# Later places in the engines' queues for three pieces of work, and other loads and layouts in a retention and sparse-attention block

## Chip, cores, metric

The kernel runs on one core of a Trainium2 chip. The metric is the time of one execution on the device in microseconds (us), the median of several runs. A profile of one execution comes with it: the span of its instructions, the busy time of each engine, and what each engine waited for. The engines are called PE (TensorE, matrix products), PEld (its weight loads), DVE (VectorE), ACT (ScalarE), POOL (GpSimd) and SP (SyncE, which here only issues DMAs).

## The reference, cut to what matters

One layer over 1,024 tokens of width 1,024, all in float32:

```
h    = rms_norm(x)                      # needs the sum of squares of each token
proj = h @ w_in                         # columns split between two token mixers
group A: q, k rotated; ret = retention(q, k, v)   # 8 heads, chunk-causal, decay per head
         ret = head_group_norm(ret) * silu(gate_a)
group B: score[t, s] = sum_h w[t, h] * relu(qi[t, h] . ki[s])   # the indexer, 8 heads
         keep the 256 best keys of each token; softmax attention over these alone,
         keys and values from a latent c_kv (rms-normalised, width 128) through w_uk, w_uv
         dsa = attention * silu(gate_b)
x = x + concat(ret, dsa) @ w_out
x = x + sigmoid(rms_norm(x) @ w_ple_gate) * (p @ w_ple_proj);  out = rms_norm(x)
```

The rotations need tables of cos and sin of position times frequency, one for the retention heads (`cosr`, `sinr`) and one for the sparse group (`cosx`, `sinx`).

## The kernel before, in words

Matrix products in full float32 precision are made of three fast ones: each operand is split into a high part (ACT copies it to the fast format, `xhi`, `whi`) and a rest (`xlo` by DVE, `wlo` by POOL). The work goes through these stages.

1. **Start.** For each of 8 slices of x: load, split (L257, L258), square on ACT, add to `acc` on DVE (L266). PE runs the first projection (L300 to L302) on the slices. On DVE the angle tables (L331 to L339, a range reduction of nine steps for each of the two tables) have no place of their own: they stand between the slices' work. When `acc` is complete, PE sums it over the partitions (L365), `rsqrt` gives `rstd`, `spread` copies it to all partitions (`rstd_b`), and DVE multiplies the tables with it and rotates the first projection (L382 to L401). The rotated indexer queries and keys go to DRAM (`d_iq`, `d_ik`), with the rotary part of the attention queries (`d_qs`) and keys (`d_kp`), all issued on SP's queue.
2. **Indexer scores** (L449 to L455), six token tiles in the order 7, 6, 4, 2, 3, 5: load `qs` from `d_iq`, 8 products per tile, relu on ACT, weighted sum on DVE. Tiles 0 and 1 need no scores.
3. **Column chunks** (`n_chunk`, L472 to L474, PE work that needs only x and weights) in the order 2, 3, 0, 1: 8 token tiles each with 24 products per tile. Then `t_block`s (L310 to L312): the retention queries and keys (rotated on DVE into `d_f`), the latent (block 8, squares on ACT at L523, their sum over partitions on PE at L526), and the attention queries (blocks 9 to 11, into `d_qs`). Then chunks 4 and 5.
4. **The search for the 256th score**, bit by bit, beside stage 3: rows 2, 3, 5 on DVE (L624), rows 7, 6, 4 on ACT (L640), then `narrow` and `choose` (L685 to L689) on DVE, which write the mask `bias`.
5. **Keys and values** from the latent: `prep_v` and `prep_k` (L726 to L745); DVE makes the rests at L731 and L745. They use the memory of x and its weights, so they come when chunk 5 is done. `start_block` loads the queries `ql`, `qh` from `d_qs` into the memory of the scores, so it comes when the search is done.
6. **Retention** in 8 halves (4 head pairs, 2 halves of the sequence), two in flight, beside the attention of query blocks 0 and 1. `retention_load` fetches mask `mk`, `qk`, `vt` and gate `gt`; `retention_out` multiplies with the gate and stores to `d_mix`.
7. **Attention** of blocks 2 and 3, beside the two output projections (`project`), the gate products and the final norm.

Each engine executes its instructions in the order of its queue, and so do the DMA issues of SP. That order isn't written by hand: a scheduler at build time makes it from priorities (mostly the order in the program) and from its own estimate of when each operand is ready. A tile pool hands out buffers in that order and makes the next user wait for the last.

Of the kernel before, what the change touches and what calls it, by code (L numbers as in the profile page):

```python
# [153 lines left out]
def _body(ctx, nc, tc, ap, dbg):  # L154
    V, A, G, T, Y = nc.vector, nc.scalar, nc.gpsimd, nc.tensor, nc.sync

    def f(t):
        return t.bitcast(F32)

    def pool(name, **kw):  # L160
        return tc.tile_pool(name=name, bufs=kw.pop("bufs", 1), reuse_waits="tile", **kw)
# [28 lines left out]
    d_iq = dram.tile([2, 32, 8, S], F32, name="d_iq")  # L190
    d_qs = dram.tile([2, 64, 8, S], F32, name="d_qs")
    d_f = [dram.tile([128, 2, S], F32, name=f"d_f{g}") for g in range(4)]
# [67 lines left out]
    def add_squares(k):  # L260
        raw = raws[k // 2][:, k % 2]
        if k == 0:
            A.activation(acc, raw, AF.Square)
        else:
            A.activation(raw, raw, AF.Square)
            V.tensor_tensor(out=acc, in0=acc, in1=raw, op=OP.add)  # L266

# [8 lines left out]
    for k in range(NT):  # L276
# [7 lines left out]
        if k > 0:  # L284
            add_squares(k - 1)
    add_squares(NT - 1)
    Y.dma_start(same, ap["cst"][:, CF:CN])
# [16 lines left out]
    def t_block(b, outs):  # L304
        ws = [load_w(ap["w_t"][b, kg], 128) for kg in range(2)]
        for h in range(2):
            sl = slice(512 * h, 512 * h + 512)
            for k in range(NT):
                wh, wl = (t[:, k % 4] for t in ws[k // 4])
                T.matmul(outs[h], wh, xhi[k][:, sl], start=k == 0, stop=False)  # L310
                T.matmul(outs[h], wh, xlo[k][:, sl], start=False, stop=False)  # L311
                T.matmul(outs[h], wl, xhi[k][:, sl], start=False, stop=k == 7)  # L312

# [30 lines left out]

    angles(1, cosx)
    tables(cosx, sinx)
    angles(0, cosr)

# [64 lines left out]
    for n in range(2):  # L413
        Y.dma_start(d_qs[n, 0:16].rearrange("(x j) h t -> (j h) x t", x=2), f(xs[n])[0:64])
        Y.dma_start(d_kp[n].rearrange("(x j) t -> j x t", x=2), f(xs[n])[104:112])
# [16 lines left out]
    for i in TI:  # L432
# [7 lines left out]
        for h in range(8):  # L440
# [5 lines left out]
            for b0, b1, pb in pbs:  # L446
                for c0 in range(b0, b1, 512):
                    c1 = min(b1, c0 + 512)
                    T.matmul(pb[:, c0 - b0:c1 - b0], qs[:, h], ks[:, c0:c1], start=True, stop=True)  # L449
                A.activation(rel[:, b0:b1], pb[:, :b1 - b0], AF.Relu, scale=32.0 ** -0.5)  # L450
# [10 lines left out]
    def n_chunk(c, func, place=nb):  # L461
        ws = [load_w(ap["w_n"][c, kg], 256) for kg in range(4)]
        for tg in range(2):
            for a in range(4):
# [5 lines left out]
                for k in range(NT):  # L470
                    wh, wl = (t[:, k % 2] for t in ws[k // 2])
                    T.matmul(pb[:, a % 2], xhi[k][:, tsl], wh, start=k == 0, stop=False)  # L472
                    T.matmul(pb[:, a % 2], xhi[k][:, tsl], wl, start=False, stop=False)  # L473
                    T.matmul(pb[:, a % 2], xlo[k][:, tsl], wh, start=False, stop=k == 7)  # L474
                A.activation(st[:, a % 2], pb[:, a % 2], func, scale=rstd[:, j:j + 1])  # L475
# [49 lines left out]
    for j in range(NT):  # L525
        T.matmul(pk[:, j:j + 1], cq[:, 128 * j:128 * j + 128], ones1, start=True, stop=True)  # L526
    rkv = cpool.tile([128, NT], F32, name="rkv")
# [3 lines left out]
    def q_block(b):  # L531
# [8 lines left out]
        for n, t in enumerate((hi, lo)):  # L540
            Y.dma_start(d_qs[n, 16 + 16 * b:32 + 16 * b].rearrange("j h t -> (j h) t"), f(t))

# [238 lines left out]
    def retention_load(g, hf):  # L781
        ts = slice(512 * hf, 512 * hf + 512)

        kk, qz = kks[hf], qzs[hf]
        mk = rp_.tile([128, 2, 128], F32, name="mk")
        Y.dma_start(mk, ap["cst"][:, CM + 256 * g:CM + 256 * g + 256].rearrange("p (h t) -> p h t", h=2))
# [71 lines left out]
    def retention_out(g, hf):  # L858
# [10 lines left out]
        G.tensor_tensor(out=og, in0=og, in1=rv[:, :, None].to_broadcast([128, 8, 64]), op=OP.mult)  # L869
        G.tensor_tensor(out=gt, in0=og.rearrange("p (c h) d -> p c (h d)", h=2), in1=gt, op=OP.mult)  # L870
        Y.dma_start(d_mix[4 * hf:4 * hf + 4, :, 128 * g:128 * g + 128].rearrange("j p c -> p j c"), gt)

# [7 lines left out]
    blocks = {}  # L880

    def start_block(i):
        tsl = slice(256 * i, 256 * i + 256)
        q = []
        for hh in range(4):
            if hh % 2 == 0:
                ql = dq_.tile([128, 4, 256], FR, name="ql")
                for n in range(2):
                    Y.dma_start(f(ql)[64 * n:64 * n + 64], d_qs[1, :, 2 * hh:2 * hh + 4, tsl])
            t = dq_.tile([128, 2, 256], FR, name="qh", bufs=6)  # L890
            for n in range(2):
                Y.dma_start(f(t)[64 * n:64 * n + 64], d_qs[0, :, 2 * hh:2 * hh + 2, tsl])
# [336 lines left out]
```

## Time and profile before

| | |
|---|---|
| runs of before | 828.28, 828.8, 830.05 us; median 828.8 |
| the profiled execution | 826.33 us, span of its instructions 824.5 us |
| instructions | 12686 |
| mean granted clock of PE | 0.969 of full speed |

The page shares out the span by engine. More is learnt here from the waits (an engine, a line, and what released it), from stretches of the span with busy time and granted clock, and from the instructions in order of time.

### The profile page before, as it was taken

How to read it: one execution, taken by the hardware profiler on the slowest of the kernel's cores; microseconds unless marked ns; L12 is line 12 of the kernel's file. 1: busy time of each engine (PE TensorE's matmuls, PEld its weight loads, DVE VectorE, ACT ScalarE, POOL GpSimd, SP SyncE). 2: the span in 40 equal slices, each digit the busy share in tenths (PEclk: the TensorE clock that was granted, in tenths of full speed). 3: DMA queues.
4: the chain of work that ended last, by engine and by line, in shares of the span. 5: the costliest groups of instructions: out<-in, count | busy, mean ns of one | idle time of the engine just before them, and what ended most of it. 6: DMA issues, size and time to landing. Idle time of an engine off the chain costs nothing.

```text
span 824.5 us, 12686 instructions
## 1 busy us (share of the span) xinstructions
PE 763.3 (93%) x4415; PEld 661.8 (80%) x4415; DVE 596.7 (72%) x1270; ACT 477.3 (58%) x1041; POOL 313.6 (38%) x237
## 2 busy tenths in 40 slices
PE   8979699979999979999889887999999999899995
PEld 5768699968888868998788776788878887688885
DVE  5948178999999999998768777556565655653655
ACT  7543267729995699971667565543464454334333
POOL 3725625452775544730037667520261101310110
PEclk9979899989999999999999998999999999999999
DMA  8312924221533122532647755773554446542511
GB/s 316 99 40 93 235 76 115 65 78 31 179 101 112 52 103 85 177 113 77 166 116 197 204 157 172 237 249 133 158 190 172 161 172 206 202 153 78 178 52 52
DMA packets 68159, 114.42 MB, mean 139 GB/s; under 512 B 6048, under 2 KB 37664, under 8 KB 68096
## 3 DMA queue, kind: packets, MB, share of 16 engines
q1 hardware_dynamic: 64480, 107.06, 41.9%
q10 hardware_dynamic: 3616, 6.55, 2.2%
q8 instruction: 35, 0.57, 0.3%
q14 instruction: 28, 0.23, 0.1%
HBM read 75.97 MB, written 37.62 MB: 138 GB/s over the span
## 4 chain that ended last, share of the span: by engine, by line
PE 50%; DVE 31%; ACT 5%; DMA 5%; issue 4%; POOL 2%; SPq 1%; POOLq 0%; ACTq 0%; DVEq 0%
DVE res L624 8%; PE lg L1146 6%; PE rb L1146 5%; PE rb L1076 4%; PE rb L1077 3%; PE rb L1078 3%; PE tp L937 3%; PE nb L472 2%; PE nb L473 2%; PE nb L474 2%; DMA qk<-d_f 2%; PE lg L915 1%; PE oo L973 1%; PE lg L914 1%; PE oo L972 1%
## 5 line engine op out<-in xcount | busy, mean ns | idle before, releaser
L640 ACT ACTIVATE ajunk<-key,cthr 128x1024 bf16<-128x1024 int16 (+5 forms) x96 | 95.7, 997 | 27.5 <-DVE key L601 15.0
L223 POOL TENSOR_TENSOR wlo<-wraw,whi 128x512 fp32r<-128x512 f32 (+1 forms) x58 | 88.0, 1533 | 53.6 <-ACT whi L222 53.5
L473 PE MATMUL nb<-wlo,xhi 128*128 128x256 f32 x256 | 74.5, 292 | 5.5 <-POOL wlo L223 5.5
L472 PE MATMUL nb<-whi,xhi 128*128 128x256 f32 x256 | 75.0, 295 | 2.2 <-ACT nst L475 1.5
L624 DVE TENSOR_SCALAR_CACHE_REDUCE res<-key,athr 128x384 f32<-128x384 int16 (+5 forms) x96 | 75.5, 786 | 1.8
L474 PE MATMUL nb<-whi,xlo 128*128 128x256 f32 x256 | 74.3, 291 | 0.0
L319 POOL TENSOR_TENSOR rs_y<-rs_a,mhalf 128x1 f32<-128x1 f32 (+1 forms) x26 | 27.1, 1046 | 122.8 <-DVE rs_a L318 120.3
L944 DVE TENSOR_TENSOR t<-tp,t 128x512 fp32r<-128x512 f32 (+1 forms) x72 | 45.7, 643 | 30.3 <-ACT t L943 29.9
L920 ACT ACTIVATE lm<-lm,mxv 128x128 f32<-128x128 f32 (+3 forms) x64 | 49.3, 772 | 21.4 <-DVE mxv L919 20.9
L943 ACT ACTIVATE t<-tp 128x512 fp32r<-128x512 f32 (+1 forms) x72 | 39.0, 556 | 37.8 <-PE oo L973 27.2
L310 PE MATMUL big<-xhi,whi 128*128 128x512 f32 x144 | 56.1, 392 | 0.4 <-DVE mb L384 0.4
L311 PE MATMUL big<-xlo,whi 128*128 128x512 f32 x144 | 56.2, 391 | 0.0
L473 PEld LDWEIGHTS nb<-wlo,xhi 128*128 128x128 f32 x256 | 51.1, 200 | 6.3 <-POOL wlo L223 5.7
L312 PE MATMUL big<-xhi,wlo 128*128 128x512 f32 x144 | 55.8, 390 | 0.0
L472 PEld LDWEIGHTS nb<-whi,xhi 128*128 128x128 f32 x256 | 50.9, 200 | 4.3 <-ACT nst L475 2.7
L454 DVE SCALAR_TENSOR_TENSOR sc<-rel,wi,sc 128x1024 f32<-128x1024 f32 (+5 forms) x42 | 47.3, 1129 | 7.5 <-ACT rel L450 4.9
L474 PEld LDWEIGHTS nb<-whi,xlo 128*128 128x128 f32 x256 | 51.0, 199 | 0.7
L937 PE MATMUL tp<-cst,lm 128*128 128x128 f32 x288 | 47.8, 282 | 2.9 <-DVE t L944 2.1
L916 DVE CUSTOM_DVE_ANT_0 lm<-lg,bias 128x512 f32<-128x512 f32 (+2 forms) x64 | 36.7, 585 | 13.6 <-PE tp L937 6.4
L937 PEld LDWEIGHTS tp<-cst,lm 128*128 128x128 f32 x288 | 35.2, 145 | 9.0 <-DVE t L944 3.8
L222 ACT ACTIVATE whi<-wraw 128x512 fp32r<-128x512 f32 (+1 forms) x58 | 34.9, 611 | 12.3 <-PE nb L474 3.0
L972 PE MATMUL oo<-t,vd 128*128 128x256 f32 (+1 forms) x144 | 38.6, 287 | 3.1 <-ACT t L943 2.6
(497 smaller groups left out, 2451.6 us busy)
## 6 DMA issues: line engine op xcount, KB each, us to landing
wraw<-in_w_t SPq DMA_DIRECT2D x26, 256.0 KB, 2.8
wraw<-in_w_n SPq DMA_DIRECT2D x24, 256.0 KB, 2.7
d_f<-o SPq DMA_DIRECT2D x8, 512.0 KB, 3.1
qk<-d_f SPq DMA_DIRECT2D x16, 256.0 KB, 3.5
ql<-d_qs SPq DMA_DIRECT2D x16, 256.0 KB, 5.2
qh<-d_qs SPq DMA_DIRECT2D x32, 128.0 KB, 4.8
twr<-in_w_out SPq DMA_DIRECT2D x8, 512.0 KB, 5.6
xt<-in_x SPq DMA_DIRECT2D x8, 512.0 KB, 4.1
```

What stands on the lines that cost most here:

```text
L223: G.tensor_tensor(out=lo, in0=raw, in1=f(hi), op=OP.subtract)
L310: T.matmul(outs[h], wh, xhi[k][:, sl], start=k == 0, stop=False)
L311: T.matmul(outs[h], wh, xlo[k][:, sl], start=False, stop=False)
L312: T.matmul(outs[h], wl, xhi[k][:, sl], start=False, stop=k == 7)
L472: T.matmul(pb[:, a % 2], xhi[k][:, tsl], wh, start=k == 0, stop=False)
L473: T.matmul(pb[:, a % 2], xhi[k][:, tsl], wl, start=False, stop=False)
L474: T.matmul(pb[:, a % 2], xlo[k][:, tsl], wh, start=False, stop=k == 7)
L624: V.tensor_scalar(junk, src[:, KS[i]], thr[:, n:n + 1], 0.0, op0=op, op1=OP.add, accum_out=cnt[:, n:n + 1])
L640: A.activation(junk[:, :128 * (i + 1)], src[:, KS[i]], AF.Sign, bias=self.thr[:, n:n + 1], accum_out=cnt[:, n:n + 1])
L920: A.activation(lm[:, :w], lm[:, :w], AF.Exp, bias=mx, scale=0.125, accum_out=den[:, a, h:h + 1])
L937: T.transpose(tp[:, o:o + 128], pt[a][:, ks_], ident)
L1146: T.matmul(po[c.start // 512][:, c.start % 512:c.start % 512 + c.stop - c.start], a, b[:, c], start=k == 0 and m == 0, stop=k == n - 1 and ...
```

## The change

Three edits make the scheduler keep an order. `issue_after(squares)` puts every DVE instruction of its block behind the last addition of squares in DVE's queue. `behind(ins, mark)` notes an instruction, and `mark(name, ins)` makes all that were noted under the name come after `ins`; both are PE instructions, and the edge is one of order in the queue, without a semaphore. The score products of token tiles 7 and 6 (the first two of the six) come behind the last product of tile 2 of chunk 3, and the sums of the latent's squares behind the first half of block 9.

The other edits: `d_qs` is laid out by blocks of 256 tokens, so that a query load reads longer runs and a query store writes shorter ones (the rotary part is now stored by 4 DMAs, before by 2); `mk` is loaded once for each head pair; `qk` is one DMA, before two; the product with the gate is written over `og` and not over the gate tile, and stored from there.

```
+    def behind(ins, mark):
+        marks.setdefault(mark, []).append(ins)
+
+    def mark(name, ins):
+        for x in marks.pop(name, []):
+            tc.add_manual_dep(x.ins, ins.ins.name, ... NoSync ..., reason="order of issue")
...
-    d_qs = dram.tile([2, 64, 8, S], F32, name="d_qs")
+    d_qs = dram.tile([2, 4, 64, 8, 256], F32, name="d_qs")
...
-    add_squares(NT - 1)
+    squares = add_squares(NT - 1)
...
# t_block
+                last = T.matmul(outs[h], wl, xhi[k][:, sl], start=False, stop=k == 7)
+            if h == 0:
+                mark(f"block {b}", last)
...
-    angles(1, cosx)
-    tables(cosx, sinx)
-    angles(0, cosr)
+    with tc.issue_after(squares.ins):
+        angles(1, cosx)
+        tables(cosx, sinx)
+        angles(0, cosr)
...
-        Y.dma_start(d_qs[n, 0:16].rearrange("(x j) h t -> (j h) x t", x=2), f(xs[n])[0:64])
+        for x in range(2):
+            Y.dma_start(d_qs[n, :, 8 * x:8 * x + 8].rearrange("b j h t -> (j h) b t"),
+                        f(xs[n])[0:64, x].rearrange("p (b t) -> p b t", t=256))
...
# indexer scores
-                    T.matmul(pb[:, c0 - b0:c1 - b0], qs[:, h], ks[:, c0:c1], start=True, stop=True)
+                    m = T.matmul(pb[:, c0 - b0:c1 - b0], qs[:, h], ks[:, c0:c1], start=True, stop=True)
+                    if i in TI[:2]:
+                        behind(m, "chunk 3 tile 2")
...
# n_chunk, after the 24 products of tile j
+                mark(f"chunk {c} tile {j}", last)
...
-        T.matmul(pk[:, j:j + 1], cq[:, 128 * j:128 * j + 128], ones1, start=True, stop=True)
+        behind(T.matmul(pk[:, j:j + 1], cq[:, 128 * j:128 * j + 128], ones1, start=True, stop=True), "block 9")
...
# q_block
-            Y.dma_start(d_qs[n, 16 + 16 * b:32 + 16 * b].rearrange("j h t -> (j h) t"), f(t))
+            Y.dma_start(d_qs[n, :, 16 + 16 * b:32 + 16 * b].rearrange("b j h t -> (j h) b t"),
+                        f(t).rearrange("p (b t) -> p b t", t=256))
...
# retention_load
+        if hf:
+            mk = halves[g, 0]["mk"]
+        else:
+            mk = ...  (tile and load as before)
-        for n in range(2):
-            Y.dma_start(qk[:, n], d_f[g][64 * n:64 * n + 64].rearrange("r x t -> (r x) t")[:, ts])
+        Y.dma_start(qk, d_f[g].rearrange("(n r) x t -> (r x) n t", n=2)[:, :, ts])
...
# retention_out
-        G.tensor_tensor(out=gt, in0=og.rearrange("p (c h) d -> p c (h d)", h=2), in1=gt, op=OP.mult)
-        Y.dma_start(d_mix[...], gt)
+        o4 = og.rearrange("p (c h) d -> p c (h d)", h=2)
+        G.tensor_tensor(out=o4, in0=o4, in1=gt, op=OP.mult)
+        Y.dma_start(d_mix[...], o4)
...
# start_block: ql and qh each by two loads (upper and lower half of the partitions), as before
+    def twice(dst, src):
+        src = src.rearrange("r h t -> r (h t)")
+        for n in range(2):
+            Y.dma_start(f(dst)[64 * n:64 * n + 64].rearrange("r h t -> r (h t)"), src)
```

## Rows read from the trace of the kernel before

**Rows 1.** Waits of PE, 40 to 520 us: total us, times, longest.

```profile
PE big L449 <- DMA qs<-d_iq: 6.5, 1, 6.5
PE ib L365 <- DVE acc L266: 5.3, 1, 5.3
...
PE ib L526 <- ACT cq L523: 4.5, 1, 4.5
...
PE rb L811 <- DMA qk<-d_f: 5.3, 4, 1.9
```

**Rows 2.** Stretches: length, busy us of PE, PEld, DVE, ACT, POOL; PE's granted clock; DMA share; GB/s.

```profile
48.00:52.00 4.00, 3.58 (x16) 3.49 (x16) 1.41 (x4) 3.32 (x4) 0.04 (x1) 0.50 0.01 2
52.00:56.40 4.40, 4.24 (x20) 4.24 (x21) 1.50 (x5) 3.95 (x6) 2.91 (x2) 0.50 0.04 7
...
64.00:75.00 11.00, 11.00 (x52) 9.11 (x51) 9.19 (x11) 2.39 (x4) 3.65 (x2) 1.00 0.17 71
75.00:93.00 18.00, 17.79 (x147) 17.18 (x145) 7.90 (x6) 7.95 (x13) 14.74 (x13) 1.00 0.74 191
...
99.60:104.40 4.80, 4.80 (x17) 4.23 (x18) 2.23 (x3) 2.92 (x4) 0.00 (x0) 0.51 1.08 340
...
180.00:301.00 121.00, 119.17 (x589) 100.35 (x588) 117.48 (x272) 103.39 (x288) 63.89 (x40) 1.00 0.30 96
...
387.00:396.00 9.00, 5.55 (x19) 3.88 (x20) 5.06 (x9) 4.60 (x9) 0.00 (x0) 0.91 0.91 208
...
411.00:515.00 104.00, 90.58 (x670) 82.27 (x670) 79.34 (x238) 65.25 (x153) 63.00 (x66) 0.96 0.59 168
515.00:824.50 309.50, 294.41 (x1575) 246.71 (x1573) 172.71 (x431) 135.65 (x266) 63.12 (x47) 0.99 0.47 159
```

**Rows 3.** DVE's groups, 5 to 50 us: busy us, mean ns; idle before.

```profile
L258 DVE SCALAR_TENSOR_TENSOR xlo<-xraw,vecs,xhi 128x1024 fp32r<-128x1024 f32 (+1 forms) x9 | 12.8, 1443 | 9.0 <-ACT xhi L257 9.0
L266 DVE TENSOR_TENSOR acc<-acc,xraw 128x1024 f32<-128x1024 f32 x7 | 10.4, 1487 | 0.0
```

**Rows 4.** DVE in order of time, 12 to 412 us: start, us, line, operation.

```profile
12.89 1.28 DVE L258 SCALAR_TENSOR_TENSOR xlo<-xraw,vecs,xhi 128x1024 fp32r<-128x1024 f32 x1 [1.72 <-ACT xhi L257]
...
42.35 2.29 DVE L266 TENSOR_TENSOR acc<-acc,xraw 128x1024 f32<-128x1024 f32 x1
...
48.56 0.68 DVE L339 TENSOR_SCALAR cosr<-cosr 128x1024 f32<-128x1024 f32 x1
...
62.52 1.23 DVE L369 TENSOR_TENSOR cosx<-cosx,rstd_b 128x1024 f32<-128x1024 f32 x1 [5.77 <-ACT rstd_b L355]
...
101.94 0.75 DVE L452 TENSOR_SCALAR sc<-rel,wi 128x1024 f32<-128x1024 f32 x1 [18.02 <-DMA d_g<-nst]
...
386.91 0.33 DVE L689 TENSOR_SCALAR bias<-junk 128x640 bf16<-128x640 bf16 x1
...
411.25 0.27 DVE L916 CUSTOM_DVE_ANT_0 lm<-lg,bias 128x128 f32<-128x128 f32 x1
```

**Rows 5.** SP's DMA issues in order of time, 83 to 84 us.

```profile
83.28 1.04 SPq L414 DMA_DIRECT2D d_qs<-xs  x1
```

**Rows 6.** POOL in order of time, 90 to 96 us.

```profile
91.57 3.74 POOL L223 TENSOR_TENSOR wlo<-wraw,whi 128x512 fp32r<-128x512 f32 x3 [1.67 <-ACT whi L222]
```

**Rows 7.** ACT in order of time, 386 to 389 us.

```profile
387.03 0.47 ACT L475 ACTIVATE nst<-rb,rstd 128x256 f32<-128x256 f32 x1 [4.33 <-PE rb L474]
```

**Rows 8.** DVE's groups, 387 to 412 us: busy us, mean ns; idle before.

```profile
L745 DVE TENSOR_TENSOR kk<-rb,kk 64x512 fp32r<-64x512 f32 x8 | 5.5, 689 | 2.2 <-ACT kk L743 2.2
```

**Rows 9.** Waits of SP's DMA issues over the span: total us, times, longest.

```profile
SPq L889 <- DVE bias L689: 32.1, 1, 32.1
...
SPq L793 <- DMA d_mix<-gt: 16.8, 6, 4.3
```

**Rows 10.** DMA issues over the span: count, KB each, median us from issue to landing.

```profile
qk<-d_f SPq DMA_DIRECT2D x16, 256.0 KB, 3.5
ql<-d_qs SPq DMA_DIRECT2D x16, 256.0 KB, 5.2
```

More of the change, by code (lines that the diff above doesn't have):

```diff
@@ L158, in f @@
         return t.bitcast(F32)
+    marks = {}
+    def behind(ins, mark):
+        marks.setdefault(mark, []).append(ins)
+    def mark(name, ins):
+        for x in marks.pop(name, []):
+            tc.add_manual_dep(x.ins, ins.ins.name,
+                              mybir.DependencyInfo(mybir.DependencyClass.NoSync, mybir.DependencyReason.DATA),
+                              reason="order of issue")
     def pool(name, **kw):
@@ L265, in add_squares @@
             A.activation(raw, raw, AF.Square)
-            V.tensor_tensor(out=acc, in0=acc, in1=raw, op=OP.add)
+            return V.tensor_tensor(out=acc, in0=acc, in1=raw, op=OP.add)
     w1 = []
@@ L311, in t_block @@
                 T.matmul(outs[h], wh, xlo[k][:, sl], start=False, stop=False)
-                T.matmul(outs[h], wl, xhi[k][:, sl], start=False, stop=k == 7)
+                last = T.matmul(outs[h], wl, xhi[k][:, sl], start=False, stop=k == 7)
+            if h == 0:
+                mark(f"block {b}", last)
     def rsqrt(out, ssum, n, w):
@@ L473, in n_chunk @@
                     T.matmul(pb[:, a % 2], xhi[k][:, tsl], wl, start=False, stop=False)
-                    T.matmul(pb[:, a % 2], xlo[k][:, tsl], wh, start=False, stop=k == 7)
+                    last = T.matmul(pb[:, a % 2], xlo[k][:, tsl], wh, start=False, stop=k == 7)
+                mark(f"chunk {c} tile {j}", last)
                 A.activation(st[:, a % 2], pb[:, a % 2], func, scale=rstd[:, j:j + 1])
@@ L784, in retention_load @@
         kk, qz = kks[hf], qzs[hf]
-        mk = rp_.tile([128, 2, 128], F32, name="mk")
-        Y.dma_start(mk, ap["cst"][:, CM + 256 * g:CM + 256 * g + 256].rearrange("p (h t) -> p h t", h=2))
+        if hf:
+            mk = halves[g, 0]["mk"]
+        else:
+            mk = rp_.tile([128, 2, 128], F32, name="mk")
+            Y.dma_start(mk, ap["cst"][:, CM + 256 * g:CM + 256 * g + 256].rearrange("p (h t) -> p h t", h=2))
         qk = f(s4([128, 2, 512], "qk"))
-        for n in range(2):
-            Y.dma_start(qk[:, n], d_f[g][64 * n:64 * n + 64].rearrange("r x t -> (r x) t")[:, ts])
+        Y.dma_start(qk, d_f[g].rearrange("(n r) x t -> (r x) n t", n=2)[:, :, ts])
         vt = f(s4([128, 2, 512], "vt"))[:, 0].rearrange("p (c d) -> p c d", d=128)
@@ L869, in retention_out @@
         G.tensor_tensor(out=og, in0=og, in1=rv[:, :, None].to_broadcast([128, 8, 64]), op=OP.mult)
-        G.tensor_tensor(out=gt, in0=og.rearrange("p (c h) d -> p c (h d)", h=2), in1=gt, op=OP.mult)
-        Y.dma_start(d_mix[4 * hf:4 * hf + 4, :, 128 * g:128 * g + 128].rearrange("j p c -> p j c"), gt)
+        o4 = og.rearrange("p (c h) d -> p c (h d)", h=2)
+        G.tensor_tensor(out=o4, in0=o4, in1=gt, op=OP.mult)
+        Y.dma_start(d_mix[4 * hf:4 * hf + 4, :, 128 * g:128 * g + 128].rearrange("j p c -> p j c"), o4)
     dw_s = ctx.enter_context(ExitStack())
@@ L880, in _body @@
     blocks = {}
+    def twice(dst, src):
+        src = src.rearrange("r h t -> r (h t)")
+        for n in range(2):
+            Y.dma_start(f(dst)[64 * n:64 * n + 64].rearrange("r h t -> r (h t)"), src)
     def start_block(i):
-        tsl = slice(256 * i, 256 * i + 256)
         q = []
@@ L887, in start_block @@
                 ql = dq_.tile([128, 4, 256], FR, name="ql")
-                for n in range(2):
-                    Y.dma_start(f(ql)[64 * n:64 * n + 64], d_qs[1, :, 2 * hh:2 * hh + 4, tsl])
+                twice(ql, d_qs[1, i, :, 2 * hh:2 * hh + 4])
             t = dq_.tile([128, 2, 256], FR, name="qh", bufs=6)
-            for n in range(2):
-                Y.dma_start(f(t)[64 * n:64 * n + 64], d_qs[0, :, 2 * hh:2 * hh + 2, tsl])
+            twice(t, d_qs[0, i, :, 2 * hh:2 * hh + 2])
             q += [(t[:, k], ql[:, 2 * (hh % 2) + k]) for k in range(2)]
```

## The prediction

> **What bounds the kernel now.** I read the waits of PE first, then the stretches, then DVE in order of time. PE is the busiest engine, and its waits before 400 us are few and long [rows 1]. It waits 5.3 us for the sum of squares, 6.5 us for the first indexer queries `qs`, 4.5 us for the latent's squares. [...]
>
> PE's time is not yet the kernel's. From 180 to 301 us DVE is busy 117.48 of 121 us and PE 119.17 [rows 2], both full at once. DVE ends the search at 387.2 us (its last mask, 386.91 + 0.33) [rows 4], and the query loads wait for exactly that [rows 9]. Keys and values wait for PE's last chunk, whose last result ACT takes out at 387.03 [rows 7], and take until about 411, where attention starts [rows 4]. So two queues meet at 387: PE (all projections, then 24 us of keys and values) and DVE (scores, then search). After 411 PE leads: 90.58 busy of 104 us, then 294.41 of 309.5 [rows 2]; what arrives earlier at 411 ends earlier at the end, nearly one for one.
>
> **The change part by part.**
>
> *Angle tables behind the squares.* In DVE's queue from 12.89 to 49.2 us [rows 4] there is no gap; slices, squares and both tables mix, so the order alone is changed, not the sum. After 12.89 DVE has 6 rests of about 1.44 us and 7 additions of 1.49 us left [rows 3]: 8.7 + 10.4 = 19.1, so the squares are complete near 32 us. At the slowest additions, 2.29 [rows 4], with rests as slow, it is 13 x 2.29 = 29.8, or 42.7. PE ends the first projection at about 42.7 (its 5.3 us wait ends at 48), so even the slow end leaves it no wait worth counting. The tables still end near 49, in the cover of the first projection; nothing needs them sooner, since the rotation also wants `rstd_b`, which now comes at 62.5 (DVE waits 5.77 us for it [rows 4]). `rstd` can now come some 6 us sooner; the sines on ACT, behind the tables, keep the rotation from gaining more. If ACT evacuates the first projection behind the sines, as it does now, PE starts the chunks only near 50.
>
> *Scores behind chunk 3, tile 2.* The edge puts 3 x 24 = 72 products of 0.121 us (17.79 us for 147 [rows 2]), 8.7 us, ahead of the scores. Queued behind the held score products are all later PE instructions, and ACT's relus and DVE's sums wait for them. [...] The weights of chunk 3 would not hold it: POOL does their last splits within 3.74 us of chunk 2's end [rows 6], a cost of up to 1 to 2 us. `qs` itself: 99.6 less the 6 from `rstd`, plus the two added `d_qs` stores ahead of it on SP, each 0 to 1.04 us [rows 5], about 94 to 95. So the scores start at 95 and not 99.6, and at full clock: with 2.4 us of slow products gone, less what was hidden behind DVE, I take **6 us** for DVE's start (101.94 becomes 96), with bounds 2 (PE from 50, weights late) and 9. DVE's idle 18.02 us ahead of its first score [rows 4] is where it comes from. DVE's search, being full, ends as much earlier.
>
> *Latent sums behind block 9.* 4.5 us of PE's wait and some slow clock go; block 9's first half covers ACT. On DVE's path it is worth nothing. [...]
>
> *Keys and values in the search's shadow.* Now they fill 387 to 411 us, 24 us. With PE ahead by 10 us or more of the search's new end, its products lie before that end, and what is left behind it is DVE's part: 16 rests at L745 and 8 like them at L731, 0.69 us each, 16.5 us [rows 8]. Attention then starts 17 us behind the search and not 24: **7 us**; a little more if some of it slides under the first attention, so I take **8**. Bounds: 0 (PE held back, the order kept) and 24 less the query load, 24 - 5.2 [rows 10] = 19, of which I count 15, since DVE's work must be done somewhere.
>
> *Loads of the halves.* PE waits 5.3 us for `qk` in four places [rows 1]. One DMA for two saves one issue, by the nearest row at most 1.04 us [rows 5], so up to 4 us in four places; fewer mask loads, and gate loads that no longer wait for a store (16.8 us of SP's waits [rows 9]), clear SP's queue. Query loads of 256 KB take 5.2 us, `qk` of 256 KB in longer runs 3.5 [rows 10]; so 1.7 us less where one is waited for, once, at the start of block 0, and hidden there by keys and values. I take **2**, bounds 0 and 5.3. The shorter runs of the query stores cost at most an issue of 1.04 us ahead of weight loads, whose products PE's lead covers: 0. `og` is now held until its store lands; the first output projection takes its buffers: +0.5, bounds 0 and 2.5.
>
> Sum: 6 + 8 + 2 - 0.5 = 15.5 us. The profiled execution took 826.33 us (span 824.5), 2.5 less than the median of the runs, 828.8; against the median the forecast is 828.8 - 15.5 = **813**.
>
> [...] The row first: behind its idle time after 387 us PE's clock is 0.91 over 9 us [rows 2], 0.8 us lost, so the start of keys and values already pays now; I add nothing for it. [...]
>
> **The rivals.**
>
> *DVE takes it all (821).* PE gets ahead, but the scheduler keeps keys and values behind the search, or DVE's rotations hold PE. Then only the scores' 6 us and the loads' 2 remain: 821, give or take 3. For it: 117.48 of 121 busy. Against: DVE has 24 us there with 16.5 of work.
>
> *Attention follows the queries (800).* 9 + 15 + 5 = 29 us. For it: first heads need only their own keys. Against: queues in order.
>
> [...]
>
> *Slower: the scores come late (832).* If the squares bring nothing to PE (chunks from 50 us or later, a chunk weight late on POOL or SP), chunk 2 ends at 93 as now, and 72 products and a weight wait of 1 us put the scores at 102.8. That is 3.2 us later for DVE, the search ends so much later, and with keys and values unmoved it is 828.8 + 3.2 = 832. It decides where the edge's 8.7 us exceed what PE gains ahead of it plus the 6.5 us it now idles, so where that gain is under 2.2.
>
> *The orders are as before (829).* The scheduler already placed things so. Against: the three waits.
>
> **How the numbers follow.** Chances: forecast 0.52 (own range 805 to 818), DVE takes it all 0.20, attention follows 0.10, paid in clock 0.06, late scores 0.08, no change 0.04. A difference under 0.2%, 1.7 us, can't be told from none. Faster: the first four without the slowest edge of the second, 0.86; same: the last and some of that edge, 0.05; slower 0.09. The bounds summed give 828.8 - 9 - 15 - 5.3 = 799.5 and 828.8 - 2 + 2.5 = 829.3. The range 800 to 826 leaves out half of the fastest case (0.05) and the last two (0.12).
>
> **What would show it.** Right: no PE wait for `acc`, `qs` or `cq`, and no clock of 0.5 near 50 and 100 us; the first score sum on DVE near 96; last mask near 381; first attention sum near 397; PE idle, not DVE, before it. Wrong: the evacuation of the first projection still behind the sines; PE waiting for POOL's splits in chunk 3; the search ending at 387 though the scores began early, which would put ACT's counts in its place; the time from the first attention to the end (now 413 us) growing.

## The result

The changed kernel took 818.89 us (median of 4 runs, 815.47 to 822.73), the kernel before 829.42 beside it (828.28 to 830.43): ratio 0.9886 [0.9844, 0.9928], 10.5 us or 1.1% faster. The forecast of 813 is 5.9 us too low; the range holds the result. The profiled execution of after took 815.47 us (span 813.7, against 824.5 before). Both profiled executions took some 3 us less than the medians beside them (815.47 against 818.89, 826.33 against 829.42), so a single term read from the two traces can hold as much chance.

The gain doesn't come as forecast. First the waits of PE between 36 and 115 us, after (engine, line and what released it; total us, times, longest):

```profile
PE nb L491 <- ACT nst L495: 10.5, 2, 10.0
PE nb L491 <- ACT it L375: 8.7, 1, 8.7
```

The waits for `acc` and `qs` [rows 1] are gone, and two longer ones stand in their place. The first is the evacuation of the first projection. ACT in order of time, after (start, us, line, operation, idle before):

```profile
48.70 1.06 ACT L354 ACTIVATE sinx<-cosx 128x1024 f32<-128x1024 f32 x1 [11.10 <-DVE cosx L353]
49.66 0.58 ACT L375 ACTIVATE it<-nb 128x512 f32<-128x512 f32 x1
...
98.69 0.47 ACT L495 ACTIVATE nst<-nb,rstd 128x256 f32<-128x256 f32 x1 [11.19 <-DMA d_g<-nst]
```

ACT stands 11.10 us before the sine, whose table DVE finishes only then; the evacuation `it`, whose products were done near 40 us, is queued behind it. PE waits 8.7 us for it, and chunk 2 starts at 50.3. The second wait is in the last row: ACT can't write a result of chunk 2 into a buffer `nst` (there are three) until an earlier one is stored to `d_g`. POOL, then SP's queue, after, show where that store was:

```profile
77.10 2.29 POOL L505 TENSOR_TENSOR nst<-nst,retn_b 128x512 f32<-128x512 f32 x1
```

```profile
89.81 1.90 SPq L448 DMA_DIRECT2D ks<-d_ik  x3
...
93.67 0.63 SPq L454 DMA_DIRECT2D qs<-d_iq  x1
94.34 3.37 SPq L510 DMA_DIRECT2D d_g<-nst  x6
```

Six stores of `d_g` leave together at 94.34 us, after all the stores of rotated rows and the loads of `ks` and `qs`. Each result passes through a product on POOL before its store, and the first of these products had ended at 79.39 us; in the kernel before, the first two stores left right behind it, at 79.42. What that does to DVE (its order of time, after; the lines of [rows 4]):

```profile
29.79 4.55 DVE L278 TENSOR_TENSOR acc<-acc,xraw 128x1024 f32<-128x1024 f32 x2
...
60.13 1.23 DVE L384 TENSOR_TENSOR cosx<-cosx,rstd_b 128x1024 f32<-128x1024 f32 x1 [3.44 <-ACT rstd_b L370]
...
110.37 0.75 DVE L471 TENSOR_SCALAR sc<-rel,wi 128x1024 f32<-128x1024 f32 x1 [27.44 <-ACT rel L469]
...
389.84 0.32 DVE L710 TENSOR_SCALAR bias<-junk 128x640 bf16<-128x640 bf16 x1
...
404.55 0.27 DVE L943 CUSTOM_DVE_ANT_0 lm<-lg,bias 128x128 f32<-128x128 f32 x1
```

The squares are complete at 34.3 us and not 48. The first score comes at 110.37, 8.4 us later than before, and the search ends at 390.16, 2.9 later. The attention still starts 6.7 us earlier than the 411.25 of [rows 4], because the values now lie beside the end of the search. ACT there, after (against [rows 7]):

```profile
381.04 0.48 ACT L495 ACTIVATE nst<-rb,rstd 128x256 f32<-128x256 f32 x1 [2.41 <-PE rb L493]
...
390.61 0.60 ACT L764 ACTIVATE kk<-lg 128x512 fp32r<-128x512 f32 x1 [0.93 <-PE lg L763]
391.53 0.60 ACT L764 ACTIVATE kk<-rb 128x512 fp32r<-128x512 f32 x1 [0.32 <-PE rb L763]
```

Chunk 5 ends at 381.5 and not 387.5; PE makes the values in the search's last 9 us, and behind its end remain the 16 half keys, one each 0.9 us as these rows show, 14.4 us in all, in which PE has no pause. The stretches of after (length, busy us of PE, PEld, DVE, ACT, POOL; PE's clock; DMA share; GB/s) answer to [rows 2]:

```profile
50.30:108.60 58.30, 47.77 (x313) 45.16 (x314) 22.96 (x23) 21.07 (x31) 25.37 (x20) 0.86 0.48 126
50.30:56.20 5.90, 5.90 (x27) 5.90 (x28) 1.57 (x6) 5.67 (x7) 2.05 (x2) 0.50 0.18 46
98.80:104.00 5.20, 4.78 (x22) 4.78 (x23) 0.00 (x0) 2.16 (x4) 2.39 (x2) 0.50 0.16 32
381.50:390.16 8.66, 6.35 (x25) 4.27 (x24) 8.55 (x14) 4.69 (x9) 0.00 (x0) 1.00 0.09 31
390.16:404.55 14.39, 14.39 (x67) 11.97 (x66) 11.45 (x17) 9.30 (x16) 0.00 (x0) 1.00 0.98 244
404.55:508.55 104.00, 89.28 (x672) 79.63 (x672) 76.83 (x239) 65.01 (x153) 65.73 (x67) 1.00 0.57 165
404.55:813.70 409.15, 380.58 (x2241) 323.07 (x2240) 248.03 (x668) 199.84 (x418) 128.45 (x112) 1.00 0.50 163
```

The last of them, before:

```profile
411.25:824.50 413.25, 384.74 (x2241) 328.74 (x2240) 251.80 (x668) 200.66 (x418) 126.13 (x112) 0.98 0.50 161
```

From the first attention to the end it took 413.25 us before and 409.15 after, with the same 2,241 products. PE idles as long in both (28.5 and 28.6 us) and is busy 4.2 us less, so between these two traces the difference is the clock and not a wait that went. The first 104 us of it ran at a clock of 0.96 before and at 1.00 here, with about as many products (669 and 672).

### The profile page after: what moved, and what is told of

It reads as the page before. It is cut to its first block, busy times and chain, and to the rows that moved or that the text cites. A ratio compares the mean times of both kernels' runs of the same rounds, so it can differ in the third digit from the quotient of the medians.

```text
span 813.7 us, 12654 instructions
## 1 busy us (share of the span) xinstructions
PE 755.0 (93%) x4415; PEld 653.5 (80%) x4415; DVE 587.5 (72%) x1270; ACT 476.8 (59%) x1041; POOL 312.5 (38%) x237
## 4 chain that ended last, share of the span: by engine, by line
PE 51%; DVE 31%; DMA 6%; ACT 4%; issue 4%; POOL 2%; SPq 1%; POOLq 0%; DVEq 0%; ACTq 0%
DVE res L645 8%; PE lg L1173 6%; PE rb L1173 5%; PE rb L1103 3%; PE rb L1104 3%; PE rb L1105 3%; DMA qk<-d_f 3%; PE tp L964 3%; DMA twr<-in_w_out 3%; PE nb L491 2%; PE nb L492 2%; PE nb L493 2%; DVE ad L654 2%; DVE sc L473 2%; DVE athr L656 2%
## 5 line engine op out<-in xcount | busy, mean ns | idle before, releaser
L661 ACT ACTIVATE ajunk<-key,cthr 128x1024 bf16<-128x1024 int16 (+5 forms) x96 | 95.5, 995 | 15.4 <-DVE key L622 10.5
L491 PEld LDWEIGHTS nb<-whi,xhi 128*128 128x128 f32 x256 | 52.1, 204 | 24.9 <-ACT nst L495 14.9
L323 PE MATMUL big<-xlo,whi 128*128 128x512 f32 x144 | 56.2, 390 | 0.0
L473 DVE SCALAR_TENSOR_TENSOR sc<-rel,wi,sc 128x1024 f32<-128x1024 f32 (+5 forms) x42 | 51.0, 1214 | 4.3 <-ACT rel L469 1.6
L1106 DVE TENSOR_TENSOR xt<-rb,xt 128x512 f32<-128x512 f32 x32 | 21.9, 689 | 30.3 <-PE rb L1105 25.9
```

The lines of the kernel that those rows point to most:

```text
L473: V.scalar_tensor_tensor(dst, rel[:, :w], wi[:, i, h:h + 1], dst, op0=OP.mult, op1=OP.add)
L661: A.activation(junk[:, :128 * (i + 1)], src[:, KS[i]], AF.Sign, bias=self.thr[:, n:n + 1], accum_out=cnt[:, n:n + 1])
```

## The experiments

Beside after, twelve kernels were timed, in three groups; each group ran on one chip with before beside it (828.03, 829.4 and 827.96 us), so ratios are what compares across groups. The table gives for each the ratio with its interval, and from its profiled execution, in us: the first score sum on DVE, the end of the search, the end of chunk 5 (its last result on ACT), the first attention sum on DVE, and the time from there to the end. These columns are of one execution each; for the last one note that after's is the fastest of its four runs, and that of the old loads the slowest of its six.

| kernel | median | ratio | first score | search ends | chunk 5 ends | attention starts | from there |
|---|---|---|---|---|---|---|---|
| before | | 1 | 101.94 | 387.24 | 387.50 | 411.25 | 413.2 |
| after | 818.89 | 0.9886 [0.9844, 0.9928] | 110.37 | 390.16 | 381.52 | 404.55 | 409.2 |
| no edge at all | 826.23 | 0.9979 [0.9948, 1.001] | 100.93 | 387.40 | 385.62 | 411.26 | 413.7 |
| no scores edge | 821.97 | 0.9944 [0.9909, 0.9978] | 98.02 | 386.03 | 387.18 | 406.38 | 410.8 |
| no table edge | 810.34 | 0.9795 [0.9751, 0.9839] | 105.21 | 383.85 | 373.78 | 398.71 | 409.6 |
| edges, old loads | 819.70 | 0.9892 [0.9853, 0.9931] | 110.94 | 389.77 | 380.10 | 404.28 | 415.4 |
| early evacuation | 807.27 | 0.9743 [0.9707, 0.9778] | 100.08 | 378.10 | 367.64 | 392.64 | 410.7 |
| stores by ACT | 813.72 | 0.9816 [0.978, 0.9851] | 101.45 | 381.26 | 374.42 | 395.64 | 414.6 |
| no table edge, stores by ACT | 821.23 | 0.991 [0.988, 0.9939] | 105.41 | 381.59 | 372.23 | 395.99 | 425.1 |
| search cut | 816.62 | 0.9837 [0.9803, 0.9871] | 110.12 | 377.28 | 379.65 | 399.47 | 416.3 |
| early evacuation, no scores edge | 823.38 | 0.9941 [0.9916, 0.9966] | 99.86 | 385.88 | 384.27 | 409.37 | 415.9 |
| three edits | 821.09 | 0.9918 [0.9885, 0.9952] | 105.53 | 384.93 | 376.30 | 399.32 | 418.0 |
| scores behind tile 5 | 824.34 | 0.9955 [0.9929, 0.998] | 120.77 | 412.08 | 380.10 | 421.18 | 404.2 |
| scores behind tile 0 | 809.66 | 0.9781 [0.9749, 0.9812] | 103.40 | 382.46 | 373.54 | 395.94 | 411.5 |

**Which edit carries the time.** Four kernels leave parts of the change out. No edge at all (loads and layouts alone):

```
-    with tc.issue_after(squares.ins):
+    with ExitStack():
...
-                    if i in TI[:2]:
+                    if False:
...
-        behind(T.matmul(pk[:, j:j + 1], cq[...], ones1, start=True, stop=True), "block 9")
+        behind(T.matmul(pk[:, j:j + 1], cq[...], ones1, start=True, stop=True), "never")
```

> The changed kernel without the three edges of order: only the loads, stores, layouts and the gate product are changed. If PE's path to the first attention carried the gain (it came 6.7 us earlier there, and 4.1 us more behind it), this gives back the 6.7: the first attention sum near 411 us, the total 4 us under before, about 825. By the prediction's own sizes the loads are worth 1.5 us, about 828. If the loads carried all of it, it stays near 819.

Without the scores edge (the table edge and the loads stay):

```
-                    if i in TI[:2]:
+                    if False:
                         behind(m, "chunk 3 tile 2")
```

> The changed kernel without the edge on the scores; the tables stay behind the squares. In the changed kernel DVE's first score sum came at 110.4 us, 8.4 later than before, though the queries had landed near 97. Search-path theory: the scores start near 98 to 100, the search ends some 5 to 10 us earlier, and the total falls to 810 to 814. PE-path theory: the search's end does not set the first attention, the last chunk does; that moves by what PE idles, 2 us either way, so 817 to 821.

Without the table edge (the scores edge and the loads stay):

```
-    with tc.issue_after(squares.ins):
+    with ExitStack():
         angles(1, cosx)
```

> The changed kernel without the edge on the angle tables; the scores stay behind chunk 3, tile 2. PE-path theory: the first projection ends 2.9 us later, as before, and the sums wait 5 us again, but PE still has chunk products to run in the wait for the queries; first attention 2 to 4 us later than in the changed kernel, about 822. Search-path theory (as predicted): the scores start as late or later than the 110 us of the changed kernel, the search ends past 390, and the total follows it: 824 or more.

The three edges on the layouts, loads and gate product of before (the stores and loads of `d_qs` go back with its layout):

```
-    d_qs = dram.tile([2, 4, 64, 8, 256], F32, name="d_qs")
+    d_qs = dram.tile([2, 64, 8, S], F32, name="d_qs")
...
-        if hf:
-            mk = halves[g, 0]["mk"]
...
-        Y.dma_start(qk, d_f[g].rearrange("(n r) x t -> (r x) n t", n=2)[:, :, ts])
+        for n in range(2):
+            Y.dma_start(qk[:, n], d_f[g][64 * n:64 * n + 64].rearrange("r x t -> (r x) t")[:, ts])
...
-        G.tensor_tensor(out=o4, in0=o4, in1=gt, op=OP.mult)
+        G.tensor_tensor(out=gt, in0=o4, in1=gt, op=OP.mult)
```

> The kernel before with the edges of order alone: loads, stores, layouts and the gate product as before. If the edges carry the gain up to the first attention, it keeps the 6.7 us there and loses the 4.1 behind it: about 822. If the layout and the loads carried it, it is near 829.

The loads alone bring 1.8 us, with an interval that holds 0 (0.9979 [0.9948, 1.001]), and beside the edges nothing that shows (0.9892 without them, 0.9886 with them). The edge of the scores brings 16 us by itself (826.23 to 810.34), but only 0.6% or 5 us beside the table edge (0.9944 to 0.9886). The table edge brings 4.3 us where the scores have none (826.23 to 821.97, with intervals that overlap), and costs where they have: 0.9886 against 0.9795, 0.9% or 7.5 us. That cost neither theory on record had: they gave 822 and 824 or more for the kernel without the table edge. The edge on the latent's sums has nothing in it: without it, the order of every engine's instructions is the same, beside the other edges and alone.

Where do the 16 us come from? Stretches from 43 us to the end of chunk 5, and one within it; no edge at all, then no table edge:

```profile
43.00:385.62 342.62, 320.42 (x1937) 288.84 (x1937) 297.20 (x552) 237.09 (x568) 161.13 (x104) 0.96 0.34 102
300.00:340.00 40.00, 37.66 (x180) 32.53 (x181) 38.94 (x111) 36.48 (x96) 17.41 (x11) 0.87 0.32 100
```

```profile
43.00:373.80 330.80, 315.45 (x1936) 285.21 (x1935) 281.04 (x548) 236.46 (x567) 159.88 (x104) 0.97 0.35 106
300.00:340.00 40.00, 37.75 (x227) 33.38 (x226) 38.91 (x107) 37.85 (x100) 25.25 (x18) 1.00 0.43 144
```

PE does the same products 11.8 us sooner: it idles 15.4 us and not 22.2, and is busy 5.0 us less, since it runs slow for less time (300 to 340 us: 0.87 against 1.00). Its waits of 40 to 400 us say which idle time went; no edge at all, then no table edge:

```profile
PE big L466 <- DMA qs<-d_iq: 5.1, 1, 5.1
PE ib L546 <- ACT cq L543: 4.5, 1, 4.5
...
PE nb L492 <- POOL wlo L235: 3.6, 1, 3.6
```

```profile
PE nb L491 <- ACT nst L495: 4.6, 3, 3.5
...
PE big L466 <- DMA qs<-d_iq: 1.9, 1, 1.9
PE nb L492 <- POOL wlo L235: 0.7, 2, 0.5
```

So the scores edge, and not the latent's, took away the wait for the latent's squares (`cq`), 200 us behind the place where it acts: it moved the whole order that follows. With the latent's edge and without the scores edge the wait is there, 4.7 us. Of the 16 us, the attention's start has 12.6 (411.26 to 398.71); the other 4.1 lie behind it (413.7 to 409.6), where PE idles 4.3 us less, and I haven't traced them further.

**What sets the start of the attention.** The search's end (as forecast), PE's path, or the later of the two. The changed kernel with the end of the search cut on DVE: for token tiles 6 and 4 the running count of ties and the two products behind it are left out, so their masks differ.

```
+                if i not in (4, 6):
                     V.tensor_tensor_scan(cum, eq, eq, 0.0, op0=OP.add, op1=OP.max)
                     V.scalar_tensor_tensor(eq, cum, need[:, n:n + 1], eq, ...)
                     V.scalar_tensor_tensor(eq, sc[:, KS[i]], kf_[:, n:n + 1], eq, ...)
```

> The changed kernel with the last part of the search cut for token tiles 6 and 4: the running count of ties and the two products behind it (three DVE instructions for each, 2.03 + 1.15 + 1.15 and 1.49 + 0.87 + 0.87 us) are left out, so DVE ends the search about 7.5 us earlier, near 383, and PE's work before is untouched. Three theories of what sets the start of the attention (404.55 us in the changed kernel). Later of two: 14.5 us behind the search's end or 20 us of products behind chunk 5's end (381.0), so 401 to 402, and the time 3 us less than the changed kernel's, 815 to 816. Search alone, as predicted: 397, time 811. PE alone: 404 to 405 and the time within 1.5 us of the changed kernel's 818.9.

The search ends 12.9 us earlier (the rests of the values, which stood between its rows, now follow it). ACT at chunk 5's end and DVE in order of time:

```profile
379.17 0.48 ACT L495 ACTIVATE nst<-rb,rstd 128x256 f32<-128x256 f32 x1 [2.40 <-PE rb L493]
```

```profile
376.95 0.33 DVE L711 TENSOR_SCALAR bias<-junk 128x640 bf16<-128x640 bf16 x1
380.73 0.69 DVE L753 TENSOR_TENSOR vd<-lg,vd 128x512 fp32r<-128x512 f32 x1 [3.46 <-ACT vd L752]
...
399.47 0.27 DVE L944 CUSTOM_DVE_ANT_0 lm<-lg,bias 128x128 f32<-128x128 f32 x1
```

DVE then idles 3.46 us for the first values, which come when PE has ended chunk 5. The attention starts 22.2 us behind the search and 19.8 us behind chunk 5, which itself ends 1.9 us earlier: the search let go, PE took over. 5.1 us of the 12.9 reach the attention, and the time falls by less than the intervals can tell (0.9837 against 0.9886). The table bears the rule out, with one exception in the size. In the kernels where chunk 5 ends 6.8 us or more ahead of the search, the attention starts 13.5 to 14.9 us behind the search (9.1 in the next kernel); in the others (before, no edge, the two kernels without the scores edge, the cut search) it starts 19.2 to 25.6 us behind chunk 5. PE's own price for keys and values is near 20 us (19.2 and 19.8 in the two where it is held least).

The other side of it, a search that starts late on purpose: the kernel without the table edge, its scores behind tile 5 of chunk 3.

```
-                        behind(m, "chunk 3 tile 2")
+                        behind(m, "chunk 3 tile 5")
```

> The changed kernel without the table edge (810.3 us when it ran), with the score products of the first two tiles behind tile 5 of chunk 3 instead of tile 2: 72 products of 0.121 us, 8.7 us, later. Later-of-two rule: PE's 1.9 us wait for the queries goes, the first score sum comes at 112 to 114 instead of 105.2, the search ends at 390 to 392 instead of 383.9 and the attention starts 14.5 us behind it, at 405 to 407 instead of 398.7; the time is 816 to 819. Rival (PE's path alone sets the time): chunk 5 ends no later than 373.8, the attention starts by 399, the time is 808 to 811.

DVE in order of time, then PE:

```profile
120.77 0.87 DVE L471 TENSOR_SCALAR sc<-rel,wi 128x1024 f32<-128x1024 f32 x1 [36.92 <-ACT rel L469]
...
407.21 0.67 DVE L766 TENSOR_TENSOR kk<-rb,kk 64x512 fp32r<-64x512 f32 x1
...
411.75 0.33 DVE L710 TENSOR_SCALAR bias<-junk 128x640 bf16<-128x640 bf16 x1
...
421.18 0.29 DVE L943 CUSTOM_DVE_ANT_0 lm<-lg,bias 128x128 f32<-128x128 f32 x1 [2.55 <-PE lg L942]
```

```profile
420.72 0.30 PE L941 MATMUL lg<-kk,qh 128*128 128x128 f32 x1 [1.43 <-DMA qh<-d_qs]
```

The search sets the attention again: it ends at 412.08, 32 us behind chunk 5 (380.1). But the attention starts 9.1 us behind it and not 14: the last rest of the keys, at 407.21, lies before the search's end, and PE waits for the queries, whose loads SP issues from 413.45 on. So the 14 us of the other kernels are no fixed price of the search, but PE's key products where they come behind it. The sizes were larger than expected (attention at 421.18 and not 405 to 407, time 824.34 and not 816 to 819). The scores came 15.6 us later for 8.7 us of products; PE also waited 5.2 us for `nst`, and the rest isn't traced. And the search took 291.3 us from its first score and not 278.6, with the keys' 16 rests of some 0.69 us now between its rows. The same edge behind tile 0:

```
-                        behind(m, "chunk 3 tile 2")
+                        behind(m, "chunk 3 tile 0")
```

> The changed kernel without the table edge (810.3 us when it ran), with the score products behind tile 0 of chunk 3 instead of tile 2: 48 products, 5.8 us, fewer ahead of them. The queries land when they did, so PE waits 1.9 + 5.8, some 7 to 8 us, for them. Later-of-two rule: chunk 5 ends some 5 us later, near 379, so the attention can't start before 399; the search ends at 382 to 384, which allows 397 to 399; the time is 809 to 813, near that of tile 2, since PE had 5 us of lead to give away. Rival (the gain of the scores edge grows with each product put ahead of the scores, 16 us for 72): 24 products bring a third, time 820 to 822.

809.66 us, as good as tile 2. The time is as expected, the way is not: PE waits 2.7 us for the queries and not 7 to 8, and chunk 5 ends at 373.54 and not near 379. The gain is not a matter of how many products go ahead of the scores: 24 do as well as 72.

**The two new waits.** The changed kernel with ACT's evacuation ahead of the sine (it holds only the indexer's sine; the other still went first):

```
-        A.activation(sin_t, ang, AF.Sin)
+        behind(A.activation(sin_t, ang, AF.Sin), "it0")
...
-            A.activation(it[:, 512 * h:512 * h + 512], PI[b][h], AF.Copy)
+            x = A.activation(it[:, 512 * h:512 * h + 512], PI[b][h], AF.Copy)
+        if b == 0:
+            mark("it0", x)
```

> The changed kernel with ACT's evacuation of the first projection put ahead of the two sines. In the changed kernel PE waits 8.7 us for that evacuation and, 39 us later, 10.0 us for result buffers of chunk 2 whose stores stand in SP's queue behind stores of the rotated rows. Theory (SP's queue sets): the 8.7 us wait goes, PE starts chunk 2 near 43 us and not at 50, but it meets the same stores, which leave SP near 94 to 95 us; so the wait for the result buffers grows to about 16 to 18 us, the first score sum on DVE stays at 109 to 112 us (110.37 in the changed kernel) and the time at 817 to 821. Rival (each wait costs what it lasts): the first score sum comes at 102 to 103, the time is 810 to 812.

My theory fell, and the result lies beyond the rival too (first score at 100.08 against 102 to 103, 807.27 us against 810 to 812): the best of all kernels here. ACT in order of time, PE's waits of 36 to 115 us, and SP's queue:

```profile
39.03 0.60 ACT L375 ACTIVATE it<-nb 128x512 f32<-128x512 f32 x1 [2.94 <-PE nb L314]
...
49.04 1.06 ACT L354 ACTIVATE sinr<-cosr 128x1024 f32<-128x1024 f32 x1 [8.11 <-DVE cosr L353]
50.01 0.61 ACT L234 ACTIVATE whi<-wraw 128x512 fp32r<-128x512 f32 x1
```

```profile
PE nb L493 <- ACT whi L234: 7.1, 1, 7.1
PE nb L493 <- ACT nst L497: 1.6, 2, 1.4
```

```profile
76.12 1.23 SPq L512 DMA_DIRECT2D d_g<-nst  x2
...
93.90 2.17 SPq L512 DMA_DIRECT2D d_g<-nst  x4
```

One half is evacuated at once, at 39.03 us. PE gets no further than the next weights, whose split `whi` is now what stands behind a sine (7.1 us), so of the 8.7 us little comes back there (from 39 to 50 us PE is busy 4.61 us, in the changed kernel 2.56). But two `d_g` stores now leave at 76.12 us instead of 94.34, the 10.0 us wait shrinks to 1.4, and the first score comes 10.3 us earlier. So this run doesn't price the evacuation by itself; it suggests that most of the loss hung on those stores. The direct test gives the stores of chunk 2 to another queue, with the order of PE nearly the same:

```
-                        Y.dma_start(dst[:, j - 1:j + 1], st.rearrange(...)[a2])
+                        (A if c == 2 else Y).dma_start(dst[:, j - 1:j + 1], st.rearrange(...)[a2])
```

> The changed kernel with the stores of chunk 2's results issued by ACT instead of SP. Theory (SP's queue sets): the 10.0 us wait of PE for chunk 2's result buffers goes, the 8.7 us wait for the evacuation stays, the products of chunk 3, tile 2 end near 98 us, the first score sum comes at 100 to 102, the search ends near 381, the attention starts near 396 to 397 and the time is 809 to 812. Rival (the store wait only hides a wait for the queries or for the split weights of chunk 3): PE waits 5 us and more for those instead, the first score sum stays behind 106, and the time at 816 or more.

PE's waits of 36 to 115 us:

```profile
PE nb L491 <- ACT it L375: 8.7, 1, 8.7
PE big L466 <- DMA qs<-d_iq: 3.4, 1, 3.4
PE nb L491 <- ACT nst L495: 0.3, 1, 0.3
```

The 10.0 us wait is gone and the other one stays; first score, end of search and start of attention came as expected (101.45, 381.26, 395.64). The time, 813.72, is 1.7 us above the expected range: the stretch from the attention on is 414.6 us and not 409.2. Its interval overlaps a little with that of the changed kernel (0.9816 [0.978, 0.9851] against 0.9886 [0.9844, 0.9928]), so the test rests on the traces more than on the time. The early evacuation without the scores edge:

```
-        A.activation(sin_t, ang, AF.Sin)
+        behind(A.activation(sin_t, ang, AF.Sin), "it0")
...
-                    if i in TI[:2]:
+                    if False:
```

> The changed kernel without the edge of the scores (822.0 us when it ran), with ACT's evacuation of the first projection ahead of the sine of the indexer's table. It separates what the table edge is worth once PE need not wait 8.7 us behind the sines. Later-of-two rule (attention starts 14.5 us behind the search's end or 20 us behind chunk 5's end, whichever is later): without the scores edge PE is the later one (386.7 + 20 = 406.4); PE gains about 3 us of chunk 2 at 39 to 50 us, as it did with the scores edge, so the attention starts at 403 to 405 and the time is 818 to 820. Rival (the early evacuation is worth what it was with the scores edge, 818.9 less 807.3): 810 to 811. Rival (nothing, the wait moves on whole to the weight splits behind the sines): 821 to 823.

823.38, the last of the three: without the scores edge an early evacuation brings nothing that shows (0.9941 against 0.9944). With it, the table edge and the early evacuation together bring 0.5% over no table edge (0.9743 against 0.9795), with intervals that overlap.

**Two tries at a better one, both failed.** The kernel without the table edge, with the stores of chunk 2 on ACT (the edit shown above):

> The changed kernel without the edge of the angle tables (810.3 us when it ran), with the stores of chunk 2's results issued by ACT instead of SP. Theory (SP's queue sets): PE's 4.6 us of waits for result buffers shrink to under 1.5, the first score sum comes at 101 to 103 instead of 105.21, the search ends 2 to 3 us earlier, and the time is 807 to 809, lower than any kernel so far. Rival (the stores are no longer on the path once PE has not the wait behind the sines): within 1.5 us of 810.3, as the queries are waited for instead.

The first stretch of the attention:

```profile
395.99:499.99 104.00, 89.05 (x639) 82.10 (x637) 72.47 (x215) 58.28 (x139) 58.28 (x61) 0.92 0.51 141
```

The search ends 2.3 us earlier and the attention starts 2.7 us earlier, as expected, though the first score doesn't move. The time was to be 807 to 809 and is 821.23: 15.5 us are lost behind the start of the attention (425.1 against 409.6), with longer waits of PE for `qk` (8.3 us, 3.4 without the edit) and a clock of 0.92. Which step of the new order does it was not tried. The second try puts both sines behind the second half of the evacuation, and moves stores to ACT:

```
-        A.activation(sin_t, ang, AF.Sin)
+        x = A.activation(sin_t, ang, AF.Sin)
+        if first:
+            after(x, first[0])
+        else:
+            behind(x, "it0")
...
-            Y.dma_start(d_qs[n, :, 8 * x:8 * x + 8].rearrange("b j h t -> (j h) b t"),
+            A.dma_start(d_qs[n, :, 8 * x:8 * x + 8].rearrange("b j h t -> (j h) b t"),
...
-        Y.dma_start(d_kp[n].rearrange("(x j) t -> j x t", x=2), f(xs[n])[104:112])
+        A.dma_start(d_kp[n].rearrange("(x j) t -> j x t", x=2), f(xs[n])[104:112])
```

> An attempt at a faster version, three edits on the changed kernel: both sines, not one, stand behind the evacuation of the first projection on ACT, and the stores of the rotary part of the attention queries and keys (six DMAs, 4.8 us of SP's queue ahead of the loads of the first indexer queries) are issued by ACT. If the scores' start is now set by the queries through SP's queue: the first score sum comes at 94 to 96 us instead of 100.08, the search ends near 373, the attention starts near 387, the time is 800 to 804, against 807.3 with the one sine moved. Rival (the splits of chunk 3's weights, or ACT's own queue with six more issues, hold the scores): first score sum at 99 or later, time 806 to 809.

SP's queue, then ACT with its own DMA issues:

```profile
91.50 5.66 SPq L524 DMA_DIRECT2D d_g<-nst  x4
```

```profile
77.02 1.41 ACTq L444 DMA_DIRECT2D d_qs<-xs  x2
...
80.17 3.42 ACTq L444 DMA_DIRECT2D d_qs<-xs  x2
...
85.92 0.84 ACT L509 ACTIVATE nst<-nb,rstd 128x256 f32<-128x256 f32 x2 [8.94 <-DMA d_qs<-xs]
```

The last load of `qs` leaves SP at 90.8 us and not at 93.7, but ACT is held for 8.9 us by the issues, and the stores of `d_g` stand behind the loads again, so PE waits 7.6 us for `nst`, much as in the changed kernel. First score 105.53, time 821.09: the rival, and worse than it. Of the 14.0 us between its profiled execution and that of the early evacuation, 6.7 are there at the attention's start and 7.3 behind it, not traced.

## Why the prediction was partly right

**Squares and tables: right in the event, wrong in the worth.** The squares were complete at 34.3 us (predicted 32) and the wait for `acc` went. `rstd` came, but the tables multiplied with it start at 60.13 and not 62.52, 2.4 us sooner and not 6: ACT copies the spread `rstd` only at 58.6 and 59.5 us, when PE, restarted at 50.3, has made it. The text had the condition ("if ACT evacuates the first projection behind the sines, as it does now, PE starts the chunks only near 50"), and that is what happened, at 50.3.

**Scores: the step that failed.** "So the scores start at 95", for a gain of 6 us on DVE. From PE's start at 50.3 the trace has 47.77 us busy in 58.3, so 10.5 us of waits for `nst` were missing in the text. Of the busy time some 5.3 us are slow clock (an estimate: half of the 5.90 and 4.78 us at 0.50), where the text said "at full clock"; without it the trace's products would take some 42 us. Its sign "no clock of 0.5 near 50 and 100 us" failed with it. No run shows the term of 6 us: the 2.4 us of slow products in it did not go here (4.78 us busy at 0.50 from 98.8 to 104), the first score came 8.4 us later, and at the earliest of all these kernels 3.9 sooner (98.02, no scores edge). The text counted SP's backlog only ahead of `qs`, and not that the results of chunk 2 share that queue and have three buffers. That the wait is a cost of its own is shown by moving these stores alone: the first score comes 8.9 us earlier and the attention as much.

**"DVE's search, being full, ends as much earlier": only in part.** The scores came 8.4 us late, the search ended 2.9 late; from the first score to the last mask DVE took 279.8 us and not 285.3. Its busy time there fell from 269.6 to 265.9 us, its idle time from 15.7 to 13.9, though 6 of the values' 8 rests now lie in it. I haven't traced that to one cause. The search's term is -2.9 us, where +6 was forecast.

**Keys and values in the shadow: the size right, the mechanism by half.** Forecast +8, measured 9.6: the attention starts 14.4 us behind the search, where it had started 24.0. The text had PE's products all before the search's end, and behind it DVE's 16.5 us of rests, with "PE idle, not DVE". Only the values came before it. PE in order of time, after:

```profile
385.39 0.50 PE L747 MATMUL lg<-uvh,ckh 128*128 128x512 f32 x1 [1.65 <-DVE vd L752]
```

PE waits for the values' rests, which DVE makes between the search's rows, and comes to the keys as the search ends; then it is busy 14.39 of 14.39 us, and DVE waits for it. That these 14.4 us lie near the text's 16 (17, less 1 under the first attention) is luck. PE's lead of 8.6 us came, but from the scores edge: the latent's edge has no effect. The text's list of PE's waits also left one out, 5.5 us for the split `wlo` between 112 and 180 us; after has 0.7 there.

**Loads: small, as said.** Forecast 1.5 net; alone they measure 1.8 with 0 in the interval, beside the edges 0.06%, and PE's waits for `qk` are 3.9 us, 5.3 before.

The profile's sum is then -2.9 + 9.6 + 4.1 = 10.8 us, where the last is the stretch from the attention on, 413.25 to 409.15. It is the term I trust least: that stretch lay between 409 and 425 us in thirteen of these kernels, with the same 2,241 products (404 behind tile 5, where 60 of them came earlier), and between before and after it differs in PE's clock and not in PE's waits. So the total comes as near the forecast as it does in part by luck: the search missed by 8.9 us, and 1.6 us more from keys and values and 2.6 more from that stretch than forecast made up for half of it.

**The rivals.** The late scores came, at 8.4 us and not the 3.2 given them, but didn't decide, since keys and values moved, which that rival took to stay. DVE did not take it all, the attention did not follow the queries, and the orders were not as before. That a lead is paid in clock, 0.06 of the chances, was not shown: from 381.5 to 390.16, where PE waits for DVE's rests, the clock is 1.00. The slow clock is behind the two new waits of 8.7 and 10.0 us, 0.50 at 50.3 to 56.2 and at 98.8 to 104 us, ahead of the scores; it is 1.00 from 56.2 to 58 and from 104 to 105. The two waits and the slow clock also cost PE's lead, of which some 3 us were left over by an estimate from the table (381.5 + 20 = 401.5 against 404.55).

## What to carry to other kernels

Here edges of order removed waits of 5.3 and 6.5 us, and waits of 8.7 and 10.0 us, for what was next in the queues behind them, came in their place: read the queues of ACT and SP, not only the engine that the edge is on, and count the staging buffers that their stores free. Where two queues meet, work out both arrival times and take the later; here the attention starts mostly 14 us behind the search or some 20 us behind the last chunk, and the 14 are the work that the other queue still has to do. And time each edge by itself: of three here, one brought 16 us, one took 7 back beside it, and one did nothing; with one more edge, which puts an evacuation ahead of a sine, the change is worth 2.6% and not 1.1%.

## What the runs showed of the hardware

An issue on SP isn't a fixed price: one store of `d_g` held SP for 0.36 to 1.21 us in the kernel before and for 0.36 to 0.64 in the changed one, one store of `d_qs` held SP for 0.65 to 1.02 us (changed kernel). On ACT two of them took 1.41 us at 77.02 and two 3.42 us at 80.17 (three edits). The time of a merged row is not that price: in the changed kernel the row of two `wraw` loads at 71.48, 2.69 us long, is one issue of 0.33 us at 71.48 and one of 0.33 us at 73.84. And runs of one kernel differ by up to 1.6% (before, 20 runs on one chip, 820.37 to 833.71 us), so differences under 0.5% between these kernels, with 4 to 12 runs each, are hints.
